# Low halves of the keys held twice: 128 rows in every score product of the second block

## The chip, the cores and the metric

The kernel runs on one core of a Trainium2 chip. Its engines work side by side: TensorE multiplies matrices (its weight loads are a lane of their own in the profile, PEld), VectorE (DVE) and ScalarE (ACT) do element by element work and read PSUM, the memory that TensorE writes its products to, GpSimd (POOL) does element by element work on SBUF, and SyncE (SP) issues most of the DMAs. Each engine takes its instructions in a fixed order, and semaphores tie them together. The metric is the device time of one execution in microseconds. Three runs of the kernel before took 2063.56, 2062.48 and 2062.10 us; the median is 2062.48.

A product on TensorE has a stationary operand (the weights, loaded by LDWEIGHTS) and a moving operand. Its *rows* are the partitions over which it sums; its *columns* are the elements of the moving operand per partition. A form such as `64*128 64x512` in the profile reads: weights of 64 rows and 128 columns, moving operand of 64 rows and 512 columns.

## The reference, cut to what matters

Two transformer blocks follow each other on 512 tokens of width 1024. The change lies in the second block's attention: 8 heads of width 64, which share 2 pairs of keys and values in three branches. Two branches see 512 keys (selected blocks and a window, which at this length are both causal attention over all tokens), the third sees 31 compressed keys, each made of 32 tokens by a small MLP.

```python
q = (q * (HEAD_DIM ** -0.5)).reshape(B, S, N_KV, GQA, HEAD_DIM)
kc = compress(k_c, cmp_pos_k, cmp_k_w1, cmp_k_w2)
vc = compress(v_c, cmp_pos_v, cmp_v_w1, cmp_v_w2)
s_cmp = jnp.einsum('bskgd,bnkd->bkgsn', q, kc)
p_cmp = masked_softmax(s_cmp, cmp_mask)
o_cmp = jnp.einsum('bkgsn,bnkd->bskgd', p_cmp.astype(vc.dtype), vc)
...
s_win = jnp.einsum('bcqkgd,bcmkd->bckgqm', qw, kw)
p_win = masked_softmax(s_win, win_mask[None, :, None, None])
o_win = jnp.einsum('bckgqm,bcmkd->bcqkgd', p_win.astype(vw.dtype), vw)
...
o = g[:, :, 0] * o_cmp + g[:, :, 1] * o_slc + g[:, :, 2] * o_win
```

## The kernel before

All matrices are f32. To multiply them at TensorE's faster f32 rate (the type fp32r), the kernel splits each into a high half in fp32r and a low half, the rest; `split` does it with a copy on ScalarE (L116) and a subtraction on VectorE (L117). `mm3` (L174 to L176) then sums three products: high by high, high by low, low by high.

The second block's attention packs this closer. A head has 64 dimensions, and TensorE has 128 rows. So `QS[h]` holds the high half of the scaled query in rows 0 to 63 and its low half in rows 64 to 127 (`ev_q`, L1695 and L1696). `KH` holds the high half of the keys twice, in both sets of rows: one product with 128 rows gives high by high plus low by high. `KL` holds the low half of the keys once, in 64 rows: a second product with the 64 upper rows of `QS` alone gives high by low. `ev_k` makes `KH` and `KL` from the projections f = 14 and f = 16.

`attn_run` goes through 64 units: 8 heads, 2 branches, 4 blocks of 128 queries. A unit's front is the product with `KH` (L1825), the product with `KL` (L1826), both of 128 to 512 columns by the causal block, and the mask, a bf16 product of 128 columns (L700); then VectorE takes the maximum (L702) and ScalarE the exponential (L704). Its back comes three units later: POOL scales the row (L715), TensorE transposes it (L721), ScalarE and VectorE split it (L116, L117), and after a head's four units `mm3` multiplies with the values into `po`.

The compressed branch is made for four heads at a time, `compressed(n)` for n = 0 and 1: a mask product (L1772), then for each head and query block one product with `kch` (128 rows, L1778) and one with `kcl` (64 rows, L1779), 32 columns each, softmax on VectorE and ScalarE, and a transpose into `PT4` (L1796, L1797), in which head g stands in rows 32g to 32g + 31. Its product with the compressed values (L1816) takes the 32 rows of a head, of `vcr` and of `PT4`, in plain f32, two passes, and closes the sum in `po`. `compress` makes `kch`, `kcl` and `vcr`; for the values the hidden layer stands four times side by side (the tile chV), so that all four sets of 32 rows of `vcr` hold the same values.

`compressed(0)` stands ahead of the units. Between them `fill` puts in other work every five units: the projections of the last queries (f = 10 and 11), `compressed(1)`, the transposes of the other half of the block (`mixa`) and its output product (`out_a`). The order on each engine is set when the program is built, by a scheduler that follows this order and each instruction's readiness.

Of the kernel before, what the change touches and what calls it, by code (L numbers as in the profile page):

```python
# [11 lines left out]
F = mybir.dt.float32  # L12
# [41 lines left out]
class Net:  # L54
# [1455 lines left out]
    def compress(self, ps, posn, w1n, w2n, pool, kind, dst):  # L1510


        nc, a = self.nc, self.a
        e = nc.vector
        pr = pool.tile([16, P], F, name=self.name("cpr"))
        nc.scalar.dma_start(pr, a[posn][0].rearrange("(r w) d -> r (w d)", w=2))
        pt = self.trp()
        nc.tensor.transpose(pt[:, :16], pr, self.ident[:16, :16])
        pos = pool.tile([P, 16], F, name=self.name("cps"))
        e.tensor_copy(pos, pt[:, :16])  # L1520
        B = pool.tile([P, 16, 2, 32], F, name=self.name("cB"))
        nc.gpsimd.memset(B[:, :, :, 31:32], 0.0)
        kc = pool.tile([P, S + 16], F, tag="ckc", name=self.name("ckc"), bufs=1)
        nc.scalar.copy(kc[:, :S], ps)
        for par in range(2):
            pp = slice(par * 64, par * 64 + 64)
            for kv in range(2):
                src = kc[kv * 64:kv * 64 + 64, :S].rearrange("p (n r w) -> p r n w", r=8, w=2)
                for half in range(2):
                    nc.scalar.copy(B[pp, half * 8:half * 8 + 8, kv, 0:31], src[:, :, half:half + 31, par])  # L1530
        for kv in range(2):
            e.tensor_tensor(B[:, :, kv, 0:31], B[:, :, kv, 0:31], pos[:, :, None].to_broadcast([P, 16, 31]), op=OP.add)

        def rest():
            ph = self.acc()
            w1 = a[w1n][0]
            for c in range(4):
                src = w1[c * 512:(c + 1) * 512].rearrange("(c p) n -> p c n", p=P)
                if c % 2:
                    raw = pool.tile([P, 4, 256], F, tag="craw", name=self.name("craw"), bufs=2)  # L1540
                    nc.sync.dma_start(raw, src)
                else:
                    raw = self.wraw(src, 4, 256)
                for k in range(4):
                    rp = c * 4 + k
                    nc.tensor.matmul(ph[:64, :256], B[:, rp].rearrange("p k n -> p (k n)"), raw[:, k], start=rp == 0,
                                     stop=rp == 15)
            hd = pool.tile([64, 256], F, tag="chd", name=self.name("chd"), bufs=1)
            nc.scalar.activation(hd, ph[:64, :256], AF.Gelu_apprx_tanh)
            pt = self.trp()  # L1550
            for c in range(2):
                nc.tensor.transpose(pt[:, c * 64:(c + 1) * 64], hd[:, c * P:(c + 1) * P], self.ident[:64, :64])
            w2 = pool.tile([P, 2, 2, 64], F, tag="cw2", name=self.name("cw2"), bufs=1)
            for j in range(2):
                nc.scalar.dma_start(w2[:, :, j], a[w2n][0].rearrange("(c p) d -> p c d", p=P))
            po = self.trp()
            if kind == "k":
                hT = pool.tile([P, 2, 64], F, tag="chT", name=self.name("chT"), bufs=1)
                e.tensor_copy(hT, pt[:, :128].rearrange("p (c n) -> p c n", c=2))
                for c in range(2):  # L1560
                    nc.tensor.matmul(po[:, :64], w2[:, c].rearrange("p j d -> p (j d)"), hT[:, c], start=c == 0, stop=c == 1)
                hi, lo = dst
                v = po[:, :64].rearrange("p (k n) -> p k n", k=2)
                nc.scalar.copy(hi, v)
                e.tensor_tensor(lo, v[:64], hi[:64].bitcast(F), op=OP.subtract)
                return
            hT = pool.tile([P, 2, 2, 4, 32], F, tag="chV", name=self.name("chV"), bufs=1)
            for c in range(2):
                e.tensor_copy(hT[:, c], pt[:, c * 64:(c + 1) * 64].rearrange("p (k n) -> p k n", k=2)[:, :, None, :]
                              .to_broadcast([P, 2, 4, 32]))  # L1570
            for kv in range(2):
                for c in range(2):
                    nc.tensor.matmul(po[:, kv * 64:(kv + 1) * 64], hT[:, c, kv].rearrange("p r n -> p (r n)"), w2[:, c, 0],
                                     start=c == 0, stop=c == 1)
            e.tensor_copy(dst, po[:, :128].rearrange("p (k d) -> p k d", k=2))
        return rest

    def block2(self, x3, out, pre):
# [35 lines left out]
                                channel_multiplier=1)  # L1614
        QS = [cp.tile([P, S], R, name=f"QS{h}") for h in range(8)]
        KH = [[cp.tile([P, S], R, name=f"KH{b}{n}") for n in range(2)] for b in range(2)]
        KL = [[cp.tile([64, S], R, name=f"KL{b}{n}") for n in range(2)] for b in range(2)]
        VV = [cp.tile([P, NT, 256], R, name=f"VV{i}") for i in range(2)]
        gate = cp.tile([P, NT, 24], F, name="gate")
        kch = cp.tile([P, 2, 32], R, name="kch2")  # L1620
        kcl = cp.tile([64, 2, 32], R, name="kcl2")
        vcr = cp.tile([P, 2, 64], F, name="vcr2")
        bsT = cp.tile([P, 8], F, name="bsT")
        gb_ = self.row(cp, A("gate_b")[0], 24, "gateb")
        gms, gm = self.pool("gm")
# [56 lines left out]
        def ev_k(f, ps):  # L1682
            b = 0 if f == 14 else 1
            for n in range(2):
                rows = slice(n * 64, n * 64 + 64)
                self.split(ps[rows], KH[b][n][0:64], KL[b][n])
                nc.scalar.copy(KH[b][n][64:128], ps[rows])

        sc = 64.0 ** -0.5

# [79 lines left out]
        def compressed(n):  # L1770
            ps = self.bank("at")
            nc.tensor.matmul(ps, self.identb, cm[:, None].to_broadcast([P, 4, NT, 32]), start=True, stop=False)  # L1772
            for g in range(4):
                h = n * 4 + g
                for qb in range(NT):
                    qs = slice(qb * P, (qb + 1) * P)
                    o = ps[:, (g * 4 + qb) * 32:(g * 4 + qb + 1) * 32]
                    nc.tensor.matmul(o, QS[h][:, qs], kch[:, n], start=False, stop=False)  # L1778
                    nc.tensor.matmul(o, QS[h][0:64, qs], kcl[:, n], start=False, stop=g == 3 and qb == 3)  # L1779
            v = ps.rearrange("p (a n) -> p a n", n=32)  # L1780
            mx, sm = (ap.tile([P, 16], F, tag=x, name=self.name(x), bufs=1) for x in ("cmx", "csm"))
            e.tensor_reduce(mx, v, axis=AX.X, op=OP.max)
            pc = ap.tile([P, 16, 32], F, tag="pc", name=self.name("pc"), bufs=1)
            e.tensor_tensor(pc, v, mx[:, :, None].to_broadcast([P, 16, 32]), op=OP.subtract)
            nc.scalar.activation(pc, pc, AF.Exp)
            e.tensor_reduce(sm, pc, axis=AX.X, op=OP.add)
            e.reciprocal(sm, sm)
            gv = sm.rearrange("p (g t) -> p g t", g=4)
            e.tensor_tensor(gv, gv, rv[:, None, :].to_broadcast([P, 4, NT]), op=OP.mult)
            e.tensor_tensor(gv, gv, gate[:, :, n * 4:n * 4 + 4].rearrange("p t g -> p g t"), op=OP.mult)  # L1790
            p2 = ap.tile([P, NT, 4, 32], F, tag="p2", name=self.name("p2"), bufs=1)
            e.tensor_tensor(p2.rearrange("p t g n -> p g t n"), pc.rearrange("p (g t) n -> p g t n", g=4),
                            gv[:, :, :, None].to_broadcast([P, 4, NT, 32]), op=OP.mult)
            pt = self.trp()
            for qb in range(NT):
                nc.tensor.transpose(pt[:, qb * P:(qb + 1) * P], p2[:, qb].rearrange("p g n -> p (g n)"), self.ident)  # L1796
            nc.scalar.copy(PT4[n], pt)  # L1797
# [7 lines left out]
        for h in range(8):  # L1805
# [7 lines left out]
                return pos[h]  # L1813

            def done(po, n=n, g=g, rows=rows, pair=pair):
                nc.tensor.matmul(po, vcr[g * 32:(g + 1) * 32, n], PT4[n][g * 32:(g + 1) * 32], start=False, stop=True)  # L1816
                nc.scalar.activation(osq[rows, pair], po, AF.Square)
                gcol = obT[rows, pair:pair + 1]
                nc.scalar.activation(oB[0][rows, pair], po, AF.Copy, scale=gcol)
                e.scalar_tensor_tensor(oB[1][rows, pair], po, gcol, oB[0][rows, pair].bitcast(F), op0=OP.mult,  # L1820
                                       op1=OP.subtract)

            for b in range(2):
                def scores(ps, qs, m, stop, b=b, n=n, h=h):
                    nc.tensor.matmul(ps, QS[h][:, qs], KH[b][n][:, :m], start=True, stop=False)  # L1825
                    nc.tensor.matmul(ps, QS[h][0:64, qs], KL[b][n][:, :m], start=False, stop=stop)  # L1826

                heads.append(dict(
                    scores=scores, po=po_, first=b == 0, last=False, done=done if b else lambda po: None,
# [113 lines left out]
```

## Time and profile before

| | us |
|---|---|
| median of three runs | 2062.48 |
| profiled execution, device time | 2056.24 |
| span of its instructions | 2054.5 |
| TensorE busy | 1871.3 (91%) |
| VectorE busy | 1403.1 (68%) |
| ScalarE busy | 1004.0 (49%) |
| POOL busy | 553.1 (27%) |

The span is the time from the first to the last instruction of the profiled execution; the 1.7 us beside it are the start and the end. The routed experts of the first block take most of the span; the second block begins at about 1310 us, its attention lasts from 1461 to 1631 us, and the feed-forward products follow to the end. Busy time of TensorE is no measure of how well it is fed: the products are pipelined, so the duration shown for one is longer than its distance to the next. What counts is the start to start distance.

### The profile page before, as it was taken

The numbers are of one execution on the slowest core, as the hardware profiler recorded it, in microseconds if no ns is written. First come the engines' busy times: TensorE is split into PE (matmuls) and PEld (weight loads), VectorE is DVE, ScalarE is ACT, GpSimd is POOL, SyncE is SP. The second block draws the span as 40 slices with busy tenths as digits, with TensorE's granted clock in tenths as the row PEclk, the third lists the DMA queues.
The fourth block names the chain that finished last, engine by engine and source line by source line (L and its number), as shares of the span: only waits on it lengthen the run. The fifth ranks groups of instructions, "written<-read, shape, count | busy, mean of one in ns | idle before, by whom it ended". The sixth has DMA issues, their size and how long they took to land.

```text
span 2054.5 us, 25345 instructions
## 1 busy us (share of the span) xinstructions
PE 1871.3 (91%) x8971; PEld 1431.9 (70%) x8971; DVE 1403.1 (68%) x2603; ACT 1004.0 (49%) x1456; POOL 553.1 (27%) x458
## 2 busy tenths in 40 slices
PE   7699898998989998999899989589999789999998
PEld 6477676786767666666666666377766578888886
DVE  8966776777789898888898888655455573332333
ACT  3363555345337676666666667345345432222220
POOL 6733111200543444344344343420122310000000
PEclk9899999999989999999999999789989889999999
DMA  5223314633459999999999999614210243333311
GB/s 149 62 82 98 113 62 153 211 103 121 187 202 336 346 346 337 343 335 341 327 344 342 338 344 334 177 32 119 71 42 1 82 123 94 102 92 93 102 52 41
DMA packets 175580, 368.92 MB, mean 180 GB/s; under 512 B 17548, under 2 KB 113112, under 8 KB 150872
## 3 DMA queue, kind: packets, MB, share of 16 engines
q1 hardware_dynamic: 154240, 309.19, 44.1%
q0 software_dynamic: 17920, 52.98, 10.5%
q10 hardware_dynamic: 3288, 5.07, 0.7%
q8 instruction: 73, 1.20, 0.2%
q14 instruction: 59, 0.48, 0.1%
HBM read 337.83 MB, written 37.75 MB: 183 GB/s over the span
## 4 chain that ended last, share of the span: by engine, by line
PE 62%; DVE 12%; DMA 12%; ACT 7%; issue 5%; POOL 1%; another core or an unknown queue 1%; ACTq 0%; DVEq 0%; SPq 0%; POOLq 0%
PE acc L174 17%; PE acc L175 16%; PE acc L176 16%; DMA raw<-in_w_exp_gu_dram 7%; ACT whi L116 3%; DVE wlo L117 2%; PE tr L721 1%; PE tr L1263 1%; ACT xt L116 1%; PE at L1826 1%; DVE xt L117 1%; DMA gx<-x2d,idx 1%; DMA accd<-y,idx 1%; PE po L175 1%; PE tr L292 1%
## 5 line engine op out<-in xcount | busy, mean ns | idle before, releaser
L116 ACT CAST whi<-raw 128x1024 fp32r<-128x1024 f32 (+3 forms) x292 | 410.8, 1411 | 408.4 <-PE acc L175 196.3
L117 DVE TENSOR_TENSOR wlo<-raw,whi 128x1024 fp32r<-128x1024 f32 (+3 forms) x281 | 478.3, 1705 | 167.4 <-ACT whi L116 160.0
L1311 POOL DMA_INDIRECT accd<-y,idx x63 | 127.8, 2029 | 369.0 <-DMA accd<-y,idx 91.3
L174 PE MATMUL acc<-whi,gT 128*96 128x512 f32 x512 | 212.5, 415 | 0.0
L176 PE MATMUL acc<-whi,gT 128*96 128x512 f32 x512 | 207.3, 405 | 0.0
L175 PE MATMUL acc<-wlo,gT 128*96 128x512 f32 x512 | 206.8, 404 | 0.0
L1254 POOL DMA_INDIRECT gx<-x2d,idx x64 | 161.3, 2520 | 60.8 <-PE acc L176 22.0
L117 DVE TENSOR_TENSOR xt<-raw,xt 128x2048 fp32r<-128x2048 f32 x64 | 146.5, 2289 | 14.0 <-ACT xt L116 9.4
L174 PE MATMUL acc<-xt,aT 128*96 128x512 f32 x256 | 109.6, 428 | 49.1 <-ACT aT L116 48.9
L174 PE MATMUL acc<-h3T,whi 128*128 128x512 f32 (+2 forms) x368 | 140.5, 382 | 0.2 <-ACT h3T L116 0.2
L175 PE MATMUL acc<-h3T,whi 128*128 128x512 f32 (+2 forms) x368 | 140.5, 382 | 0.1
L176 PE MATMUL acc<-h3T,wlo 128*128 128x512 f32 (+2 forms) x368 | 140.5, 382 | 0.0
L116 ACT CAST xt<-raw 128x2048 fp32r<-128x2048 f32 x64 | 122.1, 1907 | 0.3
L176 PEld LDWEIGHTS acc<-whi,gT 128*96 128x96 f32 x512 | 85.6, 167 | 36.7 <-issue 0.5
L175 PEld LDWEIGHTS acc<-wlo,gT 128*96 128x96 f32 x512 | 86.3, 169 | 33.0 <-issue 0.5
L174 PEld LDWEIGHTS acc<-whi,gT 128*96 128x96 f32 x512 | 86.4, 169 | 32.2 <-issue 0.3
L175 PE MATMUL acc<-xt,aT 128*96 128x512 f32 x256 | 104.8, 409 | 0.0
L1306 ACT ACTIVATE y<-acc,wsl 96x512 f32<-96x512 f32 x63 | 43.2, 686 | 125.9 <-PE acc L176 119.9
L174 PEld LDWEIGHTS acc<-xt,aT 128*96 128x96 f32 x256 | 42.5, 166 | 73.4 <-ACT aT L116 59.4
L117 DVE TENSOR_TENSOR gT<-tr,gT 128x384 fp32r<-128x384 f32 x128 | 68.6, 548 | 35.1 <-ACT gT L116 32.9
L176 PE MATMUL acc<-xt,aT 128*96 128x512 f32 x256 | 90.6, 395 | 0.0
L715 POOL TENSOR_SCALAR pf<-pf,amx,gate 128x128 f32<-128x128 f32 (+1 forms) x64 | 42.2, 668 | 156.1 <-DVE amx L713 121.3
(673 smaller groups left out, 4489.2 us busy)
## 6 DMA issues: line engine op xcount, KB each, us to landing
raw<-in_w_exp_gu_dram SPq DMA_DIRECT2D x128, 1024.0 KB
raw<-in_w_exp_down_dram SPq DMA_DIRECT2D x64, 1024.0 KB
raw<-in_w_in_dram SPq DMA_DIRECT2D x40, 512.0 KB
raw<-in_w_gate_dram SPq DMA_DIRECT2D x22, 512.0 KB
raw<-in_w_up_dram SPq DMA_DIRECT2D x22, 512.0 KB
raw<-in_w_down_dram SPq DMA_DIRECT2D x22, 512.0 KB
gsp<-sg POOLq DMA_DIRECT2D x16, 256.0 KB, 2.3
raw<-in_w_s_glu_dram SPq DMA_DIRECT2D x16, 256.0 KB
```

The costliest lines, as they stand in the source:

```text
L116: first = nc.scalar.copy(hi, src)
L117: return first, (eng or nc.vector).tensor_tensor(lo, src, hi.bitcast(F), op=OP.subtract)
L174: mm(out, l[0], r[0], start=start, stop=False)
L175: mm(out, l[0], r[1], start=False, stop=False)
L176: mm(out, l[1], r[0], start=False, stop=stop)
L292: nc.tensor.transpose(pt[:, c, :], x[:, (c0 + c) * P:(c0 + c + 1) * P], self.ident)
L715: nrm.tensor_scalar(pf[:, :n], pf[:, :n], mx[:, 2:3], h["gate"](qb), op0=OP.mult, op1=OP.mult)
L721: nc.tensor.transpose(pt[:, kb], pf[:, kb * P:(kb + 1) * P], self.ident)
L1254: nc.gpsimd.indirect_dma_start(out=gx, out_offset=None, in_=x2d, in_offset=bass.IndirectOffsetOnAxis(ap=idx, axis=0), bounds_check=S - 1, ...
L1263: nc.tensor.transpose(pt[:, c], gx[:, (c0 + c) * P:(c0 + c + 1) * P], self.ident[:C, :C])
L1306: nc.scalar.activation(y[:, :512], ps, AF.Copy, scale=w)
L1311: nc.gpsimd.indirect_dma_start(out=acc, out_offset=bass.IndirectOffsetOnAxis(ap=idx, axis=0), in_=y, in_offset=None, compute_op=OP.add)
```

## The change

Four edits, all in the second block:

- `KL` gets 128 partitions, and `ev_k` fills both sets of rows: for each of them a copy to `KH` and a subtraction to `KL`. The product L1826 takes all 128 rows of `QS` (it then also sums low by low).
- `kcl` gets 128 partitions, by one subtraction over all of them, and L1779 takes all rows of `QS`.
- `vcr` becomes a tile of four slots, set to zero by POOL; slot g is filled in rows 32g to 32g + 31 alone, by four copies on VectorE in place of one. L1816 then takes all 128 rows of `PT4` with slot g.
- The tile chV becomes part of an earlier tile (`ckc`) of the same pool, which makes up for the space.

```diff
-                e.tensor_tensor(lo, v[:64], hi[:64].bitcast(F), op=OP.subtract)
+                e.tensor_tensor(lo, v, hi.bitcast(F), op=OP.subtract)
...
-            hT = pool.tile([P, 2, 2, 4, 32], F, tag="chV", name=self.name("chV"), bufs=1)
+            hT = pool.tile([P, S + 16], F, tag="ckc", name=self.name("chV"), bufs=1)[:, :S]
+            hT = hT.rearrange("p (c k r n) -> p c k r n", c=2, k=2, r=4)
...
-            e.tensor_copy(dst, po[:, :128].rearrange("p (k d) -> p k d", k=2))
+            for g in range(4):
+                rows = slice(g * 32, (g + 1) * 32)
+                e.tensor_copy(dst[rows, g], po[rows, :128].rearrange("p (k d) -> p k d", k=2))
...
-        KL = [[cp.tile([64, S], R, name=f"KL{b}{n}") for n in range(2)] for b in range(2)]
+        KL = [[cp.tile([P, S], R, name=f"KL{b}{n}") for n in range(2)] for b in range(2)]
...
-        kcl = cp.tile([64, 2, 32], R, name="kcl2")
-        vcr = cp.tile([P, 2, 64], F, name="vcr2")
+        kcl = cp.tile([P, 2, 32], R, name="kcl2")
+
+        vcr = cp.tile([P, 4, 2, 64], F, name="vcr2")
+        nc.gpsimd.memset(vcr, 0.0)
...
-                self.split(ps[rows], KH[b][n][0:64], KL[b][n])
-                nc.scalar.copy(KH[b][n][64:128], ps[rows])
+                for c in (slice(0, 64), slice(64, P)):
+                    self.split(ps[rows], KH[b][n][c], KL[b][n][c])
...
-                    nc.tensor.matmul(o, QS[h][0:64, qs], kcl[:, n], start=False, stop=g == 3 and qb == 3)
+                    nc.tensor.matmul(o, QS[h][:, qs], kcl[:, n], start=False, stop=g == 3 and qb == 3)
...
-                nc.tensor.matmul(po, vcr[g * 32:(g + 1) * 32, n], PT4[n][g * 32:(g + 1) * 32], start=False, stop=True)
+                nc.tensor.matmul(po, vcr[:, g, n], PT4[n], start=False, stop=True)
...
-                    nc.tensor.matmul(ps, QS[h][0:64, qs], KL[b][n][:, :m], start=False, stop=stop)
+                    nc.tensor.matmul(ps, QS[h][:, qs], KL[b][n][:, :m], start=False, stop=stop)
```

The order of TensorE's instructions and of SyncE's is the same in both programs. On VectorE the order differs behind the projection f = 14. In the kernel before it reads as follows there; `KL` is the subtraction, `ug` the gating product of the other half of the block (L1713), whose input `acc` is one of the five PSUM banks of the projections, and `rss` the first step of its norm.

```order
L117 TENSOR_TENSOR KL_12900<-acc_13694,KH_12896 64x512
L1713 SCALAR_TENSOR_TENSOR ug<-acc_13725,bsT,ug 128x4x64 x2
L1713 SCALAR_TENSOR_TENSOR ug<-acc_13730,bsT,ug 128x4x64
L117 TENSOR_TENSOR KL_12901<-acc_13694,KH_12897 64x512
L1713 SCALAR_TENSOR_TENSOR ug<-acc_13730,bsT,ug 128x4x64
L1713 SCALAR_TENSOR_TENSOR ug<-acc_13735,bsT,ug 128x4x64 x2
L1713 SCALAR_TENSOR_TENSOR ug<-acc_13740,bsT,ug 128x4x64 x2
L1506 TENSOR_SCALAR rss_13865<-rss_13865 128x1
```

At the same place in the changed program, where L1713 has become L1718:

```order
L117 TENSOR_TENSOR KL_12900<-acc_13695,KH_12896 64x512
L1718 SCALAR_TENSOR_TENSOR ug<-acc_13728,bsT,ug 128x4x64 x2
L117 TENSOR_TENSOR KL_12900<-acc_13695,KH_12896 64x512
L1718 SCALAR_TENSOR_TENSOR ug<-acc_13733,bsT,ug 128x4x64 x2
L117 TENSOR_TENSOR KL_12901<-acc_13695,KH_12897 64x512
L1718 SCALAR_TENSOR_TENSOR ug<-acc_13738,bsT,ug 128x4x64 x2
L117 TENSOR_TENSOR KL_12901<-acc_13695,KH_12897 64x512
L1718 SCALAR_TENSOR_TENSOR ug<-acc_13743,bsT,ug 128x4x64 x2
L1506 TENSOR_SCALAR rss_13873<-rss_13873 128x1
```

Each pair of gating products now has a subtraction in front of it, and the last pair stands behind four subtractions in place of two. Behind the projection f = 16 the two further subtractions stand between the steps of the norm in the same way.

On POOL one instruction is added, ahead of the low halves `wlo` of the weights for the first projection of the second block. `cmaskf` and `rowvis` are the masks of the compressed branch. In the changed program the place reads:

```order
L117 TENSOR_TENSOR wvg_12828<-raw_12839,wvg_12827 128x560
L1609 MEMSET cmaskf 128x128
L1615 MEMSET rowvis 128x4
L1627 MEMSET vcr_12909 128x512
L1610 AFFINE_SELECT cmaskf<-cmaskf 128x128
L1616 AFFINE_SELECT rowvis<-rowvis 128x4
L1612 MEMSET cmaskf 128x4
L1613 CAST cmask<-cmaskf 128x128
L117 TENSOR_TENSOR wlo_12847<-raw_12844,whi_12846 128x1024
```

Without the row of `vcr` it is the order of the kernel before.

## Rows read from the trace of the kernel before

**Rows 1.** Stretches: us; busy of TensorE, its loads, VectorE, ScalarE, POOL; clock; DMA.
```profile
1466.80:1473.60 6.80, 6.80 (x20) 5.35 (x20) 2.59 (x5) 2.72 (x6) 0.00 (x0) 0.50 0.29 77
1504.40:1514.60 10.20, 10.20 (x32) 7.37 (x33) 4.41 (x7) 2.94 (x5) 0.00 (x0) 0.50 0.08 21
1518.00:1528.20 10.20, 9.34 (x30) 6.08 (x31) 6.63 (x15) 5.83 (x17) 2.48 (x4) 0.50 0.17 53
1528.20:1612.50 84.30, 84.30 (x452) 57.87 (x450) 47.49 (x129) 43.53 (x129) 23.00 (x38) 1.00 0.07 18
1612.50:1631.00 18.50, 15.64 (x78) 9.71 (x77) 7.84 (x23) 7.59 (x22) 4.80 (x8) 0.91 0.27 92
```

**Rows 2.** The chain that ended last, 1461 to 1631 us, by line.
```profile
by line: PE at L1826 13.0%; PE tr L721 12.7%; PE acc L174 7.2%; PE at L1825 7.1%; PE acc L176 7.1%; PE acc L175 7.0%; PE po L175 6.5%; PE po L176 6.1%; PE po L174 5.8%; PE at L700 5.6%; PE po L1816 4.9%; PE at L1779 4.7%; PE at L1778 4.4%; 
```

**Rows 3.** TensorE in order of time, score products: start us, us, names.
```profile
1571.41 0.48 PE L1825 MATMUL at<-KH,QS 128*128 128x512 f32 x1
1571.73 0.60 PE L721 MATMUL tr<-ident,pf 128*128 128x128 f32 x4
...
1582.30 0.47 PE L1825 MATMUL at<-KH,QS 128*128 128x512 f32 x1
1582.70 0.50 PE L1826 MATMUL at<-KL,QS 64*128 64x512 f32 x1
1583.13 0.23 PE L700 MATMUL at<-maskb,identb 128*128 128x128 bf16 x1
...
1583.75 0.32 PE L1826 MATMUL at<-KL,QS 64*128 64x128 f32 x1
1584.01 0.23 PE L700 MATMUL at<-maskb,identb 128*128 128x128 bf16 x1
```

**Rows 4.** The same view, two products of 512 columns and 128 rows.
```profile
1579.15 0.39 PE L175 MATMUL acc<-wlo,mixA 128*128 128x512 f32 x1
1579.38 0.40 PE L176 MATMUL acc<-whi,mixA 128*128 128x512 f32 x1
```

**Rows 5.** TensorE in order of time, compressed scores; last, products of one column.
```profile
1461.17 0.39 PE L176 MATMUL acc<-hT,wlo 128*128 128x512 f32 x1
1461.40 0.39 PE L1772 MATMUL at<-cmask,identb 128*128 128x512 bf16 x1
...
1462.37 0.28 PE L1778 MATMUL at<-kch,QS 128*128 128x32 f32 x1
1462.58 0.28 PE L1779 MATMUL at<-kcl,QS 64*128 64x32 f32 x1
...
1469.08 0.47 PE L1825 MATMUL at<-KH,QS 128*128 128x128 f32 x1
...
1500.42 0.37 PE L1778 MATMUL at<-kch,QS 128*128 128x32 f32 x1
...
1509.78 0.79 PE L1825 MATMUL at<-KH,QS 128*128 128x512 f32 x1
...
1632.04 2.39 PE L1838 MATMUL tr<-ones,osq 128*128 128x1 f32 x19 [0.68 <-ACT osq L1817]
```

**Rows 6.** TensorE in order of time, products of plain f32.
```profile
1439.12 1.89 PE L1546 MATMUL acc<-craw,cB 128*64 128x256 f32 x8
...
1576.48 1.07 PE L1816 MATMUL po<-PT,vcr 32*64 32x512 f32 x2
```

**Rows 7.** Other engines: tile KL, POOL and VectorE in time, TensorE's waits.
```profile
1326.30 10.48 POOL L117 TENSOR_TENSOR wlo<-raw,whi 128x1024 fp32r<-128x1024 f32 x4 [7.28 <-DMA raw<-in_w_in_dram]
...
L117 DVE TENSOR_TENSOR KL<-acc,KH x4: 676/688/693, 1425.7 to 1437.6; 64x512 fp32r<-64x512 f32 x4
...
1442.17 0.29 DVE L1559 COPY chT<-tr 128x128 f32<-128x128 f32 x1 [2.56 <-PE tr L1552]
...
1466.16 1.23 DVE L117 TENSOR_TENSOR wlo<-raw,whi 128x1024 fp32r<-128x1024 f32 x1 [1.90 <-ACT whi L116]
...
PE tr L1796 <- DVE p L1792: 1.8, 1, 1.8
```

## Prediction

> **What bounds the kernel now.** I read four views. First the busy times by stretch from 1466.8 us on [rows 1]: this is the second block's attention, some 170 us of the 2054.5. In the stretch 1528.2 to 1612.5 TensorE is busy for all 84.3 us, while VectorE has 47.5 and ScalarE 43.5. The reader is also to see the granted clock: 0.50 of full in three stretches (the lower level, 1.2 GHz), otherwise 1.00 (2.4 GHz). Second the chain of waits of this part [rows 2]: it runs over TensorE nearly everywhere, and its largest single line is L1826, the second score product, which has only 64 rows. So TensorE is the bound here, and what it does not do in this stretch is time won, until another engine is late. Third the instructions of TensorE in order of time [rows 3 to 6], where I look at start to start distances, not at durations, since the durations overlap. Fourth the other engines at the places where the change adds work [rows 7].
>
> **What a change of row count costs.** A product of 512 columns whose successor also has 128 rows starts that successor 0.23 us later [rows 4]. L1826 with 64 rows and 512 columns starts its successor, the 128-row mask product L700, after 0.43 us (1582.70 to 1583.13) [rows 3]: leaving the 64 rows costs 0.20. L1825 with 512 columns, which follows the short L700, has a distance of 0.32 when a 128-row transpose comes next (1571.41 to 1571.73) and 0.40 when the 64-row L1826 does (1582.30 to 1582.70): entering costs 0.08. That the mask is bf16 isn't the reason: L176 to the bf16 mask L1772, both of 128 rows, takes 0.23 (1461.17 to 1461.40) [rows 5].
>
> The row says 0.20 and 0.08 for a pair of changes. The Trainium skill, page "TensorEngine Tiling (Array Packing)", section "Key Properties", says that a change of tiling mode, and not of the tile alone, drains TensorE; a 64-row product between 128-row ones is two such changes. By that rule both gaps go when every product has 128 rows, and the trace agrees as far as it shows the gaps only there.
>
> **The change part by part**, against the profiled execution (2056.24 us).
>
> *Scores.* 64 pairs of L1825 and L1826 (8 heads, 2 branches, 4 query blocks; 16 of each width). Entering: 64 x 0.08 = 5.1 us. Leaving: for 256, 384 and 512 columns I take 0.20 each, 48 x 0.20 = 9.6. For 128 columns the distance is 0.26 (1583.75 to 1584.01) [rows 3], and what stays is the weight load: products of one column with 128-column weights come every 0.12 us (19 in 2.39, the last with its 0.25 of tail) [rows 5]. So 16 x 0.14 = 2.2. Sum 16.9 us. The KL product itself has the same number of columns, thus the same time. Bounds: 0 if the gap is not due to the rows, and 17.9 if all leave 0.20.
>
> *Compressed scores.* Each head group has 16 pairs, all 32 products alternate between 128 and 64 rows, at 0.21 us (1462.37 to 1462.58). Group 0 goes from 1461.40 to 1469.08, 7.7 us, group 1 from 1500.42 to 1509.78, 9.4 us, of which four transposes take some 0.5 [rows 5]. With 128 rows throughout the weight load of 0.12 decides: 32 x 0.12 = 3.8 and 4.4 us. Gains 3.9 and 5.0, sum 8.9.
>
> *Clock behind it.* In both groups the granted clock fell in the middle of these thin products, 5.4 and 4.0 us after their start, and came back only after the dense work behind them, at 1473.6 and 1514.6 [rows 1]. The groups will be over in about 4 us, so I expect the clock to stay up. Then 1469.1 to 1473.6 and 1509.8 to 1514.6 run at 2.4 GHz: half of 4.5 and of 4.8, 4.7 us. Bounds 0 and 9.8 (if the stretch 1518.0 to 1528.2 also stays up, 5.1 more; I count that at nothing, since TensorE sits idle before it, see below).
>
> *Compressed values.* The product of L1816 (two passes, 32 rows) takes 1.07 us for 512 columns, its tail included; eight passes of the same f32 kind with 256 columns and 128 rows take 1.89, so two of 512 at most 0.94 [rows 6]. With an entry of 0.08 that is 0.2 x 8 heads = 1.7 us. Bounds 0 and 2.5. Zero rows add no columns.
>
> *Added, VectorE.* Four more subtractions of KL at 0.69 us [rows 7], 2.8 us, and they alternate with ScalarE's copies, so that each waits for the one before. The order shows the second one of each pair ahead of the gating products ug of L1713, which release PSUM and feed the norms. All of this lies behind the dense projections of 1425 to 1461, and the cover is the 2.56 us that VectorE sat idle before the copy chT at 1442.17 [rows 7]. If it is used up, TensorE waits at L1561 for that copy, in its order before the remaining products of the compressed values. 2.8 us of work and some waits against 2.56: I take 0.7 us lost, bounds 0 and 3. The three extra copies of vcr fall into VectorE's pause before the queries (nothing).
>
> *Added, POOL.* One memset of 128x512 stands in front of the four wlo subtractions of the gate weights, and its own wait is for work of the routed experts that ended long before. POOL sat idle 7.28 us for a DMA there, and four subtractions of twice the size took 10.48, 2.6 each [rows 7], so the memset is below 2.6 and hidden. If the DMA were there at once, it would cost its duration. The kcl part is one instruction as before, and the tile hT of the values takes the place of an earlier one whose readers are long done. No DMA is added, and TensorE's order is unchanged.
>
> *What is late next.* (a) After group 0 TensorE comes to the query weights some 3.9 us earlier: 1461.40 + 3.8, plus two score units at full clock (1.0), gives 1466.2, and its third product, 0.46 later, needs wlo, which is done at 1466.16 + 1.23 = 1467.4 [rows 7]: 0.7 us given back. (b) After group 1 TensorE already waits 1.8 us for the softmax of group 1 (L1796) [rows 7]; that chain doesn't shrink with TensorE, and less work stands beside it: 2 us given back. (c) In the last stretch TensorE is busy for 15.6 of 18.5 us [rows 1]; there the chain through ScalarE, VectorE and POOL decides: 1 us. (d) Elsewhere VectorE goes from 56% to about 68% of its stretch: 1 us.
>
> Sum: 16.9 + 8.9 + 4.7 + 1.7 = 32.2 us, less 0.7 + 0.7 + 2 + 1 + 1 = 5.4, so 26.8, rounded to 27. The profiled execution would come to 2029. The median of the runs shown is 2062.48, 6.2 above the profiled one; the change doesn't touch what makes that difference, so I predict 2062.5 - 27 = 2035.5 us.
>
> **Rivals.**
> - *The softmax becomes the bound.* The clock gain stays out (4.7) and the units wait on VectorE and ScalarE for a third of the score gain (6): 16 us, 2046. For it: the last stretch, where TensorE already waits. Against it: 47.5 and 43.5 of 84.3 us [rows 1].
> - *The clock stays up in 1518.0 to 1528.2 too.* 5 us more, 2030.5. Against it: the idle time before it grows.
> - *Weight loads no longer hide.* If loads of the same rows could not run beside a product, each L1826 and its successor would wait for a 0.12 load: 0.24 in place of 0.28, 64 x 0.04 = 2.6 us, and the compressed products would have 0.15 in place of 0.21, 3.8 us; with 1.7 that is 8, 2054. Against it: products of 512 columns with new 128-row weights each come every 0.23 [rows 4], with no room for 0.12. The Trainium skill, page "TensorE: Matmul & The Clock Gate", section "The mechanism", states such a rule: a load overlaps a running product only when the row group differs; elsewhere on the page a background buffer is an exception, and rows 4 agree with the exception.
> - *It doesn't do what it says.* The gaps come from something else that L1826 and the compressed products share, such as reading QS a second time. Nothing is won and VectorE's 0.7 is lost: 2063.
> - *Slower: the clock.* TensorE done sooner waits in every unit for the softmax, and the granted clock falls in 1528.2 to 1612.5, where it is now 1.00 throughout. Some 70 us of work remain there; each microsecond of it at 1.2 GHz costs one more, so from 27 us on it is a loss, and for all of it 2035.5 + 70 = 2105. For it: the clock fell after the 1.8 us wait at L1796. Against it: nothing in these 84 us comes near to that wait, and VectorE would have to go from 56% to full.
>
> **How the numbers follow.** Forecast 0.70 (its own range 2029 to 2042), softmax 0.15, more clock 0.07, loads 0.03, nothing 0.02, slower 0.03. A difference of 0.2% (4.1 us) is about what can be told from none. The first four lie below it: faster 0.95; within it the fifth, 0.02; slower 0.03. The range reaches from the case with more clock to the softmax case: 2027 to 2046.
>
> **What would show it.** Right: L1826 to L700 at 0.23 for 512 columns, the pair L1825 to L1826 at 0.32; the compressed products every 0.12, with cmx about 4 and 5 us earlier relative to their start; clock 1.00 behind both groups; chT at most 1 us later. Wrong: the distances of L1826 stay at 0.43; or they shrink and TensorE shows new idle time in front of the transposes L721, released by POOL or VectorE; or a granted clock of 0.5 between 1528 and 1612.

## The result: faster, 8 us short of the forecast

| | before | after |
|---|---|---|
| median, us (6 runs each, taken side by side) | 2063.88 | 2043.88 |
| lowest to highest run | 2062.10 to 2071.89 | 2038.71 to 2050.94 |
| profiled execution, device time | 2056.24 | 2041.58 |
| span | 2054.5 | 2039.9 |
| TensorE / VectorE busy | 1871.3 / 1403.1 | 1851.5 / 1408.0 |

The ratio of the times is 0.9898, 95% interval 0.9879 to 0.9918: about 20 us less. The forecast was 27 us and 2035.5; of the 8.4 us between, 7.0 are the gain and 1.4 the kernel before, whose median is 2063.9 here and was 2062.5 in the runs shown.

In what follows *the stage* is the time from the first mask product of the compressed branch (L1772, now L1777) to the row of one-column products that waits for osq (L1838, now L1843). It took 170.6 us before (1461.40 to 1632.04 [rows 5]) and takes 151.0 now (1466.39 to 1617.43): 19.6 less. Its start lies 5.0 us later, of which about 0.5 belongs to the change (below); the rest arises ahead of 1400 us, where the change adds only a memset of 0.5 us on POOL that nothing waits for. Over all profiles of this study that start lay anywhere from 1461.4 to 1474.9. So the profiled executions differ by less than the medians, and I compare stages.

First the busy times by stretch after the change, as in [rows 1]: the stretches at half clock, and the one at full clock between them.

```profile
1469.20:1476.00 6.80, 6.80 (x26) 5.82 (x26) 3.12 (x7) 3.66 (x7) 0.00 (x0) 0.50 0.31 87
1503.30:1510.10 6.80, 6.80 (x29) 5.39 (x28) 4.53 (x8) 2.92 (x5) 0.17 (x1) 0.50 0.25 76
1513.50:1517.00 3.50, 3.28 (x14) 2.71 (x14) 1.88 (x6) 2.59 (x11) 1.01 (x2) 0.51 0.47 143
1517.00:1605.70 88.70, 85.07 (x500) 61.45 (x500) 56.04 (x154) 51.87 (x152) 27.25 (x44) 1.00 0.12 37
1605.70:1609.10 3.40, 3.15 (x13) 2.25 (x13) 0.72 (x3) 0.53 (x2) 1.59 (x3) 0.50 0.00 0
1612.50:1615.90 3.40, 3.40 (x12) 2.42 (x13) 0.00 (x0) 0.00 (x0) 0.00 (x0) 0.50 0.00 0
```

TensorE is still the bound: 85.1 of 88.7 us in the long stretch at 2.4 GHz. But it no longer fills it, and the granted clock is down to 0.50 (1.2 GHz) in both thin groups, as before: 23.9 us of the stage in five stretches, against 30.7 in four.

The chain of waits from 1466.4 to 1617.4 answers to [rows 2]. The second score product, 13.0% of the chain before as L1826, is 5.5% as L1831, and VectorE's maximum of a unit (amx) now stands among the larger shares.

```profile
by line: PE tr L721 12.7%; PE acc L176 8.1%; PE acc L174 8.0%; PE po L175 7.8%; PE acc L175 7.6%; PE at L1830 7.3%; PE po L176 7.1%; PE po L174 6.4%; PE po L1821 5.5%; PE at L1831 5.5%; PE at L1784 2.8%; PE at L1783 2.7%; DVE amx L702 2.7%;
```

TensorE in order of time answers to [rows 3, 5, 6] (start us, us, names):

```profile
1466.39 0.39 PE L1777 MATMUL at<-cmask,identb 128*128 128x512 bf16 x1
...
1466.64 0.26 PE L1784 MATMUL at<-kcl,QS 128*128 128x32 f32 x1
1466.76 0.26 PE L1783 MATMUL at<-kch,QS 128*128 128x32 f32 x1
...
1469.53 0.37 PE L1784 MATMUL at<-kcl,QS 128*128 128x32 f32 x1
1469.75 0.37 PE L1783 MATMUL at<-kch,QS 128*128 128x32 f32 x1
...
1471.03 0.45 PE L1830 MATMUL at<-KH,QS 128*128 128x128 f32 x1
...
1477.95 0.27 PE L1831 MATMUL at<-KL,QS 128*128 128x128 f32 x1
1478.07 0.23 PE L700 MATMUL at<-maskb,identb 128*128 128x128 bf16 x1
...
1563.62 1.07 PE L1821 MATMUL po<-PT,vcr 128*64 128x512 f32 x2
...
1568.88 0.48 PE L1830 MATMUL at<-KH,QS 128*128 128x512 f32 x1
1569.20 0.39 PE L1831 MATMUL at<-KL,QS 128*128 128x512 f32 x1
1569.43 0.23 PE L700 MATMUL at<-maskb,identb 128*128 128x128 bf16 x1
...
1617.43 3.98 PE L1843 MATMUL tr<-ones,osq 128*128 128x1 f32 x26 [0.68 <-ACT osq L1822]
```

Read the distances. L1830 to L1831 with 512 columns 0.32 (was 0.40), L1831 to the mask 0.23 (was 0.43), with 128 columns 0.12 (was 0.26). The thin products come every 0.12, but from 1469.2 on, at half clock, every 0.22; the first group takes 4.6 us (1466.39 to 1471.03), not 7.7. The product with the compressed values takes 1.07 us, as before.

TensorE's waits, first in the stage, then ahead of it (1425 to 1461 us):

```profile
PE tr L721 <- DVE PT L117: 1.9, 2, 1.2
PE tr L1801 <- DVE p L1797: 1.8, 1, 1.8
PE po L175 <- DVE PT L117: 0.9, 3, 0.4
...
PE at L1830 <- ACT pf L704: 0.4, 1, 0.4
PE tr L721 <- POOL pf L715: 0.4, 1, 0.4
...
PE tr L1561 <- DVE chT L1559: 0.3, 1, 0.3
```

To close the account I summed the start to start distances of all of TensorE's instructions in the stage, idle time apart:

| us in the stage | before | after | change | forecast |
|---|---|---|---|---|
| low score products, and what stands directly ahead of them (64 each) | 43.0 | 25.8 | -17.2 | -16.9 |
| compressed scores with their masks (66) | 16.0 | 8.8 | -7.2 | -8.9 |
| compressed values (16) | 8.4 | 8.3 | -0.1 | -1.7 |
| other TensorE work (513): transposes, projections, values | 90.9 | 91.0 | +0.2 | -4.7 (clock) |
| masks and the other high score products (77): waits without a mark | 6.5 | 9.1 | +2.6 | |
| idle | 5.9 | 8.0 | +2.1 | +4.7 with the row above |
| sum | 170.6 | 151.0 | -19.6 | -27.5 |

### The profile page after: what moved, and what is told of

It is laid out like the page before. It is cut to its first block, busy times and chain, and to the rows that moved or that the text cites. A ratio compares the mean times of both kernels' runs of the same rounds, so it can differ in the third digit from the quotient of the medians.

```text
span 2039.9 us, 25354 instructions
## 1 busy us (share of the span) xinstructions
PE 1851.5 (91%) x8971; PEld 1425.2 (70%) x8971; DVE 1408.0 (69%) x2610; ACT 1003.7 (49%) x1456; POOL 557.8 (27%) x459
## 4 chain that ended last, share of the span: by engine, by line
PE 57%; DVE 16%; DMA 13%; ACT 7%; issue 5%; POOL 1%; another core or an unknown queue 1%; DVEq 0%; ACTq 0%; SPq 0%; POOLq 0%
PE acc L174 16%; PE acc L175 15%; PE acc L176 15%; DMA raw<-in_w_exp_gu_dram 5%; DVE wlo L117 3%; ACT whi L116 2%; DMA accd<-y,idx 2%; DMA gx<-x2d,idx 2%; PE tr L721 1%; PE tr L1263 1%; ACT xt L116 1%; DVE xt L117 1%; PE po L175 1%; PE po L176 1%; PE po L174 1%
## 5 line engine op out<-in xcount | busy, mean ns | idle before, releaser
L116 ACT CAST xt<-raw 128x2048 fp32r<-128x2048 f32 x64 | 122.1, 1908 | 0.4
L116 ACT CAST gT<-tr 128x384 fp32r<-128x384 f32 x128 | 58.2, 480 | 55.5 <-PE tr L1263 55.5
```

Source lines behind the costliest of these rows:

```text
L116: first = nc.scalar.copy(hi, src)
```

## The experiments

Twelve runs in four steps. "Half clock" in the table at the end counts up to the end of the stage; in the expectations it is counted to the first one-column product.

**One part at a time.** e1_keys is the kernel before with the edits of `KL` alone:

```diff
-        KL = [[cp.tile([64, S], R, name=f"KL{b}{n}") for n in range(2)] for b in range(2)]
+        KL = [[cp.tile([P, S], R, name=f"KL{b}{n}") for n in range(2)] for b in range(2)]
...
-                    nc.tensor.matmul(ps, QS[h][0:64, qs], KL[b][n][:, :m], start=False, stop=stop)
+                    nc.tensor.matmul(ps, QS[h][:, qs], KL[b][n][:, :m], start=False, stop=stop)
```

> Only the edit of the keys (KL with 128 rows), compressed keys and values as before. The stretch from the first compressed product to the first product L1838 took 170.6 us before and 151.0 with all edits. If the two edits of the scores add up, this one gives what the distances of L1825 and L1826 lost, 14 us, less what the softmax takes back: stretch 156 to 160, whole kernel 10 to 15 us under the kernel before. Rival: the gain depends on the thin products as well (through the clock behind them): stretch above 162.

Measured: stage 156.5, 14.1 less; median 2050.32 (4 runs), ratio 0.9925, interval 0.9898 to 0.9952. The row of the score products falls to 25.0 us.

e2_compressed has the edits of `kcl` alone:

```diff
-        kcl = cp.tile([64, 2, 32], R, name="kcl2")
+        kcl = cp.tile([P, 2, 32], R, name="kcl2")
...
-                    nc.tensor.matmul(o, QS[h][0:64, qs], kcl[:, n], start=False, stop=g == 3 and qb == 3)
+                    nc.tensor.matmul(o, QS[h][:, qs], kcl[:, n], start=False, stop=g == 3 and qb == 3)
```

> Only the compressed keys with 128 rows. Theory: the thin products come every 0.11 instead of 0.21, each group is over 3 to 5 us sooner, stretch 162 to 165; score pairs keep 0.43 and 0.40. Rival: the clock falls at another moment and gives the gain back, stretch above 167.

Measured: stage 163.5, 7.1 less; 27.3 us of half clock in place of 30.7.

e3_values has the edits of `vcr` and chV alone:

```diff
-                nc.tensor.matmul(po, vcr[g * 32:(g + 1) * 32, n], PT4[n][g * 32:(g + 1) * 32], start=False, stop=True)
+                nc.tensor.matmul(po, vcr[:, g, n], PT4[n], start=False, stop=True)
```

> Only the values in the zero-padded tile. My prediction had 1.7 us for this. The trace of the changed kernel shows the same distances as before (0.15 ahead of the product, 0.48 and 0.52 behind its passes), so I now expect no gain: stretch 170 to 171.5. Rival: some gain that the other edits hide, stretch 169.

Measured: stage 170.9, 0.2 more, with the product exactly as long as in [rows 6]:

```profile
1583.11 1.07 PE L1821 MATMUL po<-PT,vcr 128*64 128x512 f32 x2
```

So the parts add up about: 14.1 + 7.1 - 0.2 = 21.0 against 19.6 for all. Each of these is one execution, and two executions of one kernel differ by up to 3.8 us in this stage (e5 below), so the agreement within 1.4 us is in part luck. The rows of the account part the edits without that: the low score products fall from 43.0 to 25.0 us in e1 and stay at 43.0 in e2, the compressed scores fall from 16.0 to 7.5 in e2 and take 16.9 in e1. Two parts carry the gain, the third nothing.

**Which property of the rows counts.** e4_rows96 is the changed kernel, its low score product cut to 96 rows (it leaves out part of the low by low terms):

```diff
-                    nc.tensor.matmul(ps, QS[h][:, qs], KL[b][n][:, :m], start=False, stop=stop)
+                    nc.tensor.matmul(ps, QS[h][0:96, qs], KL[b][n][0:96, :m], start=False, stop=stop)
```

> All edits, but the second score product takes 96 of the 128 rows (low by low is summed over half of its rows only, which is far below the rounding of the sum). If what costs is the change of the array's tiling (64 rows make another tiling, 96 do not), the distances are those of the changed kernel, 0.23 to 0.24 behind the 512 columns, stretch 150 to 152. If it is any difference in the number of rows between neighbours, they are 0.43 again and the stretch is 162 to 166.

Measured: stage 151.2, as with 128 rows, and the distance to the mask is 0.24 (with 64 rows it was 0.43):

```profile
1584.61 0.39 PE L1831 MATMUL at<-KL,QS 96*128 96x512 f32 x1
1584.85 0.23 PE L700 MATMUL at<-maskb,identb 128*128 128x128 bf16 x1
```

A different number of rows costs nothing by itself; 64 rows between products of 128 do. By the Trainium skill, page "TensorEngine Tiling (Array Packing)", section "Tiling Modes", sets of 64 rows are a mode of their own and a change of mode drains the engine. The distances of [rows 3] and this run agree; the price, 0.08 and 0.20 us, is the trace's. e3 does not fit: in plain f32 the product with 32 rows pays no such price.

e5_no_values takes the edits of the values out of the changed kernel again; e6_zero in addition fills the second half of `KL` with zeros (it leaves low by low out):

```diff
+        for b in range(2):
+            for n in range(2):
+                nc.gpsimd.memset(KL[b][n][64:128].bitcast(F), 0.0)
...
-                for c in (slice(0, 64), slice(64, P)):
-                    self.split(ps[rows], KH[b][n][c], KL[b][n][c])
+                self.split(ps[rows], KH[b][n][0:64], KL[b][n][0:64])
+                nc.scalar.copy(KH[b][n][64:128], ps[rows])
```

> Edits of the score products and of the compressed score products as in the changed kernel; the compressed values as in the kernel before (32 rows, one slot, no zeros, one copy, the tile chV back). Measured from the first product of the compressed mask to the row of one-column products that waits for osq: 170.6 us before, 151.0 changed. Theory: the product with 128 rows of zeros is worth nothing (0.48 and 0.52 us between its passes in both kernels), so this kernel shows 151.0 within 0.3 and a median within 1 us of the changed one. Rival: the edit is worth the 1.7 us of my forecast and something else hid it; then 152.7.

> As e5, but the second set of rows of KL holds zeros, written by POOL long before, and not the low half a second time: four subtractions less on VectorE, the same products on TensorE (low by low is left out, as in the kernel before). Theory: the gap of TensorE depends on the rows of the tile, not on their contents, so the products L1831 keep 0.23 to the mask; only the 0.4 us that VectorE's later copy chT cost in front of the compressed stage goes, which lies outside of the 151.0. Median 0 to 1 us below e5. Rival: VectorE's four subtractions push more than that (the 0.7 of my forecast and its upper bound 3): 1 to 3 us below.

Measured: e5 145.6, outside of both numbers, e6 149.0. Both run the same products in the same order, so the 3.5 us between them can't come from the values. The other work of TensorE makes 3.0 of them (87.1 and 90.1 us), and what differs there is the clock. In e5's profile two stretches at 0.50 are left, and the clock stays at 1.00 to the end:

```profile
1470.70:1477.40 6.70, 6.70 (x25) 5.62 (x25) 3.50 (x6) 3.76 (x7) 0.00 (x0) 0.50 0.28 78
1504.80:1508.10 3.30, 3.30 (x14) 2.27 (x14) 2.70 (x4) 1.22 (x2) 0.00 (x0) 0.50 0.00 0
1508.30:1613.00 104.70, 97.00 (x572) 69.53 (x570) 64.31 (x176) 59.86 (x171) 31.15 (x49) 1.00 0.14 41
```

What e6 was meant for, it showed: with four subtractions fewer VectorE is idle again ahead of chT, as in [rows 7], and TensorE no longer waits for chT at L1561. VectorE's wait there (1425 to 1461 us):

```profile
DVE chT L1559 <- PE tr L1552: 2.5, 1, 2.5
```

From the first transpose of the block's normed input to the start of the stage it is 121.5 us before, 122.1 after, 122.2 in e5 and 121.7 in e6: the four subtractions cost about 0.5 us. The medians, 2041.85 and 2042.23 (4 runs each), can't tell that.

**Whose doing the clock is.** e10_dense puts dense products in place of the thin ones:

```diff
-                    nc.tensor.matmul(o, QS[h][:, qs], kch[:, n], start=False, stop=False)
-                    nc.tensor.matmul(o, QS[h][:, qs], kcl[:, n], start=False, stop=g == 3 and qb == 3)
+                    nc.tensor.matmul(ps, QS[h][:, qs], KH[0][n], start=False, stop=g == 3 and qb == 3)
```

> As e5, but in both compressed groups each pair of thin products (32 columns) is replaced by one product of QS with all 512 columns of KH into the same bank: 16 products of 0.23 us in place of 32 of 0.11, so a block of about the same 3.7 us, dense. It leaves the compressed scores out and puts other values in their place. Theory: the thin products set the granted clock off, so in this kernel it stays at 1.00 through the first group and behind it. Rival: the clock falls at the same place for another reason (what follows the block, or the dense 40 us ahead of it): half clock from about 3 us after the start of the block, as in the changed kernel.

Measured: the clock holds through the first group and behind it, though TensorE waits 0.2, 0.5 and 0.6 us there. Behind the second group TensorE now waits 4.1 us for p, and there it falls. With 6.8 us of half clock, the least of all runs, the stage still takes 148.9 us, since 13.1 of them are idle.

```profile
1474.60:1484.60 10.00, 8.63 (x40) 6.05 (x40) 5.70 (x11) 5.18 (x10) 0.45 (x1) 1.00 0.39 107
1518.50:1525.30 6.80, 4.37 (x18) 3.41 (x18) 3.39 (x8) 3.08 (x9) 1.00 (x2) 0.50 0.22 77
```

So in the first group it is the thin products that set the clock off (one execution, against a fall there in each of those with a thin block), and in the changed kernel a block of 4.6 us in place of 7.7 doesn't prevent it. For the second group this run can't tell, since its own wait comes in between.

after_again and e5_again are two kernels run once more.

> The changed kernel once more. Between the profiles of the changed kernel and of e5, whose TensorE does the same instructions in the same order, the granted clock differs: half clock 20.5 and 10.3 us in this stage, 151.0 and 147. Theory: this is not a matter of the kernel, the clock falls or stays in the second half of the block according to the moment at which the execution comes there; then this profile can show either, and any value from 146 to 151 with the half clock to match, and a device time that differs as much. Rival: e5's other slots made the difference; then this profile repeats 20.5 us and 151.0 within 0.5.

> The kernel of e5_no_values once more (compressed values as before). Its first profile had 10 us of half clock up to the first one-column product and 145.6 us to the row that waits for osq; e6, with the same products in the same order, had 20.5 and 149.0, and the changed kernel 20.5 and 151.0, then 17 and 150.6. Theory: the clock's fall around the second group is a matter of the execution, not of the slot of the compressed values, so this profile lies anywhere from 145 to 151, and outside of 145.6 within 0.5 more likely than not; in every case the time goes with the half clock, about 0.5 us for each. Rival: the form of the compressed values decides, then 145.6 within 0.5 and 10 us of half clock again.

Measured: 150.6 with 20.5 us of half clock, and 149.4 with 22.0. e5_again decides: one kernel, 10.2 and 22.0 us of half clock, 145.6 and 149.4 us, so 0.3 us for each microsecond, less than the 0.5 that I gave. The two executions were on different chips, but e6, on the chip of e5's first, had 20.5 with the same products, so the chip alone is not the reason. after_again alone would not have decided: its first group lost the clock for 3.4 us less, but TensorE came to the query weights too early and waited 0.7 us for them in the stage (whi 0.2, wlo 0.5). e5_again at half clock (4.9 us more follow at the stage's end):

```profile
1473.20:1479.90 6.70, 6.37 (x17) 4.17 (x15) 4.26 (x8) 4.44 (x10) 0.45 (x1) 0.50 0.30 78
1507.30:1510.60 3.30, 3.30 (x14) 2.41 (x13) 3.30 (x7) 1.06 (x3) 0.00 (x0) 0.50 0.10 7
1514.10:1520.90 6.80, 6.25 (x26) 4.58 (x25) 4.78 (x12) 5.16 (x15) 1.05 (x3) 0.50 0.28 80
```

These runs show one thing more: the fall needn't come inside the block. In after_again the first block ran at full clock and was over after 3.8 us (1470.50 to 1474.33), as the prediction wanted it; the clock still fell, 1.9 us behind it. First TensorE's rows, then the stretches:

```profile
1470.50 0.39 PE L1777 MATMUL at<-cmask,identb 128*128 128x512 bf16 x1
...
1474.33 0.31 PE L1830 MATMUL at<-KH,QS 128*128 128x128 f32 x1
```

```profile
1470.50:1476.20 5.70, 5.41 (x42) 4.73 (x41) 2.25 (x3) 2.23 (x3) 0.00 (x0) 1.00 0.35 92
1476.30:1479.60 3.30, 2.99 (x8) 2.25 (x9) 2.18 (x6) 2.04 (x4) 0.00 (x0) 0.50 0.57 154
```

In e5_again both blocks were over, after 3.8 and 4.1 us, when it fell 0.7 us behind each of them, with no wait of TensorE in between.

**Attempts at a better version.** e7_spread places the thin products in parts of 8 between units:

```diff
-        compressed(0)
...
-        fill = (each(queries, (10, 11)) + each(compressed, (1,)) + each(mixa, range(NT))
-                + each(out_a, range(NT)))
+        parts = lambda n: [lambda g=g: part(n, g) for g in range(4)]
+        fill = (each(queries, (10,)) + parts(0) + each(queries, (11,)) + parts(1) + each(mixa, range(NT)) + each(out_a, range(NT)))
```

> As e5, but the 32 thin products of a compressed group stand in four parts of 8, each between two score units, in place of one block. Theory: the granted clock falls because the thin products stand in one block that TensorE alone can't fill, so with parts of 0.9 us it does not fall: half clock from 20.5 us to 10 or less in this stage, and 151.0 becomes 145 to 148. Rival 1: the clock falls anyway (any stretch of short products or a wait sets it off): 20 us of half clock, 150 to 152. Rival 2: the softmax of a group comes later and its transposes wait longer: half clock gone, but 151 or more. By the clock theory the median is 3 to 6 us below e5.

Measured: from the first unit, which here comes ahead of the first mask product, 158.0 us (1469.24 to 1627.19), with 15.3 idle; from that mask product, as the expectation counts, 152.3. The median is 2050.24 (6 runs), ratio 0.9921, interval 0.9891 to 0.9950. Without the block TensorE does three units and then stands still for the query weights, and the clock is down (from 1472.3 us) before the first thin product:

```profile
1470.26 0.23 PE L700 MATMUL at<-maskb,identb 128*128 128x128 bf16 x1
1473.88 0.80 PE L174 MATMUL acc<-hT,whi 128*128 128x512 f32 x1 [3.39 <-ACT whi L116]
```

The first thin block is the cover of that load. So the half clock isn't gone, and 152.3 us comes near to the first rival, in which a wait sets it off; the run says nothing on thin parts by themselves.

e8_lag4 is e5 with a lag of four units:

```diff
-    B2L = 3
+    B2L = 4
```

> As e5, but a unit's back (scaling, transposes, split) follows its front after four units and not three. Theory: TensorE's new waits in the units (idle 4.9 us before, 7.0 changed; the distance behind the mask 6.1 and 9.4 in sum) come from the two banks of the transposes and the scores, which VectorE and ScalarE empty too late, so a longer lag changes nothing: within 1 us of e5. Rival: they are the latency of one unit's chain through ScalarE and POOL; then the longer lag takes 2 to 4 us off.

Measured: stage 154.8 with 12.0 us idle and 23.9 of half clock, so worse in this execution, which neither theory said; the median 2044.48 (4 runs) is not distinct from e5's. TensorE's waits for VectorE's splits and for free score banks grow:

```profile
PE tr L721 <- DVE PT L117: 4.0, 4, 1.9
PE at L1825 <- ACT pf L704: 2.2, 6, 0.5
```

So a longer lag doesn't take the new waits away, as it would if they were the latency of one unit; since it brings waits of its own, the run doesn't settle the point. That all of them are the banks is argued, not shown.

e9_mix leaves the first group a block and mixes the second with dense products:

```diff
-            self.proj_feat(hT, KD, w_in, [f], ev_q)
+            self.proj_feat(hT, KD, w_in, [f], ev_q, mid=(lambda k: thin(1, k // 4, k % 4)) if f == 11 else None)
...
-        fill = (each(queries, (10, 11)) + each(compressed, (1,)) + each(mixa, range(NT))
+        fill = (each(queries, (10, 11)) + each(some, range(4)) + each(turn, (1,)) + each(mixa, range(NT))
```

> As e5, but the second compressed group's 32 thin products are mixed with dense ones: half of them in pairs between the products of the query projection f = 11, half in fours of pairs between score units, and the transposes of its softmax come three units later. The first group stays one block. Theory: thin products set the clock off when nothing dense stands between them, and the 1.8 us wait of the transposes for p is a matter of order. Then around the second group no half clock is left (10 us of it in the profile of the changed kernel, 3.4 us in e5's) and no wait for p: stage of 151.0 becomes 144 to 147, median 4 to 7 us below e5. Rival 1: the clock falls there all the same: 149 to 151. Rival 2: as in e7 new waits take the gain: 149 or more with idle time of TensorE over 9 us.

Measured: stage 146.8, the wait for p gone and 13.7 us of half clock (it still falls once behind the second group, at 1511.0); but others wait in its place, and the median, 2041.73 (6 runs), ratio 0.9889, interval 0.9868 to 0.9910, is that of e5.

```profile
PE at L1852 <- ACT pf L706: 2.0, 2, 1.4
PE acc L174 <- ACT whi L116: 1.5, 1, 1.5
PE po L175 <- DVE PT L117: 1.5, 3, 1.0
```

| run | stage, us | half clock, us | idle, us |
|---|---|---|---|
| before | 170.6 | 30.7 | 5.9 |
| e3_values | 170.9 | 30.7 | 5.9 |
| e2_compressed | 163.5 | 27.3 | 5.8 |
| e1_keys | 156.5 | 23.9 | 7.5 |
| after / after_again | 151.0 / 150.6 | 23.9 / 20.5 | 8.0 / 8.7 |
| e4_rows96 | 151.2 | 23.9 | 7.9 |
| e6_zero | 149.0 | 20.5 | 7.2 |
| e5_no_values / e5_again | 145.6 / 149.4 | 10.2 / 22.0 | 7.8 / 7.4 |
| e9_mix | 146.8 | 13.7 | 8.6 |
| e7_spread (from its first unit) / e8_lag4 | 158.0 / 154.8 | 27.3 / 23.9 | 15.3 / 12.0 |
| e10_dense (without the compressed scores) | 148.9 | 6.8 | 13.1 |

e5, e6 and e9 lie some 2 us below the changed kernel in the median; the intervals overlap, so none is shown to beat it.

## Why the prediction held, and where it was off

The sign and the main mechanism were right, and 2043.9 lies inside the range of 2027 to 2046, but at its upper end and 2 us above the forecast's own range. Of the 27.5 us in the stage 19.6 came; the 7.9 between them are the clock 4.9, the compressed scores 1.7 and the values 1.6, less 0.3 at the scores.

- *Scores*, 16.9: 17.2 measured. Leaving came to 10.8 against 11.8, entering to 6.4 against 5.1, since behind a transpose, where 10 of the 64 stand, the entry cost 0.18 and not 0.08.
- *Compressed scores*, 8.9: 7.2. The distance of 0.12 was right; that the whole block would run at 2.4 GHz was not. 2.8 us of it still ran at half clock, which is 1.4.
- *Clock behind them*, 4.7: this step failed. "The groups will be over in about 4 us, so I expect the clock to stay up" took the time to the fall (5.4 and 4.0 us) for a constant, and took for granted that a block that is over by then keeps the clock. Both were wrong, and the second group, 4.4 us by my own sum, wasn't over at 4.0 either. The clock fell 2.8 us after the start of the first group and 3.6 after that of the second, and in other executions of the same products in the same order 2.8 to 5.8; after_again and e5_again lost it although the block was over. e10 shows for the first group that the thin products cause it, the repeated kernels that its moment is the execution's. The other work of TensorE thus takes 91.0 us as before. In e5's first execution, where 10.2 us of half clock were left in the stage, the same work takes 87.1: the term is real, but it is a draw, and here it wasn't won.
- *Compressed values*, 1.7: nothing. I took the 0.08 of entering 64 rows, and compared two passes of 512 columns with eight of 256. In plain f32 a product with 32 rows and one with 128 take the same (e3), and the distance ahead of it doesn't change either.
- *KL on VectorE*, 0.7: about 0.5. The cover of 2.56 us was used up, as worked out, and chT came just late.
- *What is late next*, 4.7: 4.7 in the sum, at other places, so the size is luck. The wait for p stayed at 1.8, so (b) cost nothing and not 2; (a), 0.7, is absent in the profile of after and 0.7 in after_again. In their place the units wait: 2.1 us more idle, and 2.6 us in the distances behind masks and high products, which carry no mark of a wait. For the masks the trace shows that they are waits: ten of the 64 have their successor 0.2 us or more behind them, in place of 0.04 to 0.07, against three before, and it starts 0.04 to 0.14 us after ScalarE or VectorE ended what it waits for (four times the exponential L704). For the high products it is argued. e1 has 1.6 and 2.4 of them, so they come with the faster scores.
- The rivals: the softmax rival at 2046 is the nearest number, and its first half (no clock gain) came true; its second (6 us of waits beyond those booked) didn't, since the waits came to the 4.7 that were booked. More clock didn't come: the third stretch of half clock shrank from 10.2 to 3.5 us, but one of 3.4 at 1605.7 is new. That nothing is won is refuted by L1831 to the mask, 0.23 in place of 0.43, which also shows that loads still hide. For the slower case I had named half clock between 1528 and 1612. By the figure 1605.7 lies there, but it is 11.7 us ahead of the stage's end, where 1612.5 was 19.5 ahead of it: it belongs to the last stretch, and in the units the clock held from 1517 to 1605.

## What to carry to other kernels

Look in TensorE's order for products of 64 rows between products of 128, and take their start to start distance: here 0.28 us more for each at 2.4 GHz, above the 0.23 that its 512 columns take, and filling up the rows won nearly all of it. Don't book a clock that "will stay up" because a thin block gets shorter: it falls inside the block or up to 1.9 us behind it, at a moment that differs between executions, so count it as a range. A block that looks wasteful can be the cover of a load (here the query weights): before it is broken up, see what would be waited for without it.

## What was not expected of the hardware

- A 96-row product between 128-row ones costs nothing extra (0.24 us for 512 columns); a 64-row product costs 0.28 more.
- A 32-row product in plain f32 costs no more than one of 128 rows (1.07 us for two passes of 512 columns), though it too has other rows than its neighbours. So the price of a change does not show in every form of product.
- The same kernel had 10.2 and 22.0 us of half clock in one stage in two executions, on two chips. The Trainium skill, page "TensorE: Matmul & The Clock Gate", section "What's actually happening", says that the chip's look at activity runs freely and isn't started by the kernel, so that the same kernel varies from run to run; e5 and e5_again agree.
